# Four PSUM banks for products, two for linear attention's turns, x loaded two blocks ahead, four raw tiles for y

## The chip, the cores and the metric

The kernel runs on one core of a Trainium2 chip. The metric is the device time of one execution in microseconds. Engines: PE is TensorE (matmuls and, with `ident` as one operand, transposes), ACT is ScalarE, DVE is VectorE, POOL is GpSimd, SP is SyncE, whose queue issues nearly all transfers of this kernel. PSUM holds eight banks of 128 x 512 float32; every result of PE lands in one of them and has to be read by another engine before the bank can be written anew.

## The reference

A decoder block with two token mixers side by side, over 2048 tokens of width 1024 and 16 meta tokens set before them:

```python
h = jnp.concatenate([meta, x], axis=1)
u = rms_norm(h, norm_g[l])
proj = u @ w_in[l]
(g_q, g_k, g_v, g_lr, g_z, m_cq, m_ckv, m_kr, m_z,
 gate_gla, gate_mla) = jnp.split(proj, cuts, axis=-1)
gk = jax.nn.log_sigmoid(g_lr @ gla_gate_w[l] + gla_gate_b[l]) / GLA_GATE_NORMALIZER
o_a = gla_chunked(q, k, v, gk)
o_a = rms_norm(o_a, gla_norm_g[l]).reshape(B, L, GLA_VW)
y_a = (o_a * jax.nn.silu(g_z)) @ gla_proj[l]
o_b = mla_attention(m_cq, m_ckv, m_kr, ...)
y_b = (o_b * jax.nn.silu(m_z)) @ mla_proj[l]
merged = jax.nn.sigmoid(gate_gla) * y_a + jax.nn.sigmoid(gate_mla) * y_b
out = rms_norm(h + merged @ w_out[l], final_norm_g)[:, N_META:]
```

`gla_chunked` is linear attention with a decay: a state of 128 x 256 for each of four heads is carried over chunks of tokens. All arithmetic is float32; the kernel splits each operand into a high and a low part (`_hi`, `_lo`) and makes one product of three matmuls (`mm3`, lines 45 to 47).

## The kernel before

Everything is one program for one core. The code is written in an order that follows the data, and a scheduler places the instructions of each engine statically; a tile of a pool can be handed out again when its readers have been placed, so the number of buffers of a pool decides which waits there are.

**Input phase.** `Natural(g)` takes half of the tokens, eight blocks of 128 rows. `norm(b)` loads a block of x and norms it, `turn(b)` transposes it on PE into two banks `pt`, `place(b)` copies these as high and low parts into the operand tiles `y11` to `t4` (ACT and DVE, for some of them POOL). `run()` multiplies the blocks by columns of `w_in` that come in five pieces of about 300 columns: pieces 0 and 1 in a loop over the blocks, beside their loading and placing; pieces 2 to 4 each after the other, over all blocks. `load_w` brings a piece as eight raw tiles, which ACT (`w_hi`, line 171) and DVE (`w_lo`, line 172) convert. A product of a block and a piece is 24 matmuls of 128 x 296 or 304. Here `prep(next)` stands ahead of the two products of a block, so that a block is loaded, normed, turned and placed one turn ahead.

**Pairs.** The other columns of `w_in` go pair by pair: seven products of 12 matmuls of 128 x 512, each in a bank `acc` of the pool `a_ps`. After every product a tick lets the work beside the pairs run a step: first `latents` (MLA's small projections), then `gla`. In the first half (g = 0) latents run beside 8 pairs and `gla` beside 11, in the second beside 5 and 13; one or two pairs remain as a tail.

**Linear attention.** `gla` has 32 units, one for 256 tokens of a head; `FIRST` = 13 of them belong to the first half. A unit is a generator that yields at steps: load q and k; `xp` (the gate, one matmul, in the bank of `b_pm`), then the chain of log-sigmoid, prefix sums and decays up to `kp` on ACT, DVE and POOL; three yields; `kt` (the transposed `kp`, two transposes in the one bank of `b_pt`) with its readers `kt_hi` (ACT) and `kt_lo` (DVE), and `at` (in `b_pm`); then twice `o` and `su` with the state's update; the scale and `on`; two yields; `ot` (four transposes of `on`, again in the bank of `b_pt`). Three to four units are open at a time, so steps of different units stand beside each other.

**GlaProj.** It multiplies y, eight tiles `y` of 128 x 512 for each of four groups of tokens, by `gla_proj`. `load_y` loads a raw tile `y_raw` (two buffers, line 1010) and converts it (`y_hi` on ACT, line 1014; `y_lo` on DVE, line 1015). Three tiles of the next group can be held in advance; the others follow as the last row of products releases their places.

Attention and the output phase come behind and are not touched.

Of the kernel before, what the change touches and what calls it, by code (L numbers as in the profile page):

```python
# [19 lines left out]
P = 128  # L20
# [15 lines left out]
FIRST = 13  # L36
# [115 lines left out]
def phase_ab(tc, ident, x, meta, norm_g, w_in, gate_w, gate_b, gate_b_cols, gnorm_cols, S,  # L152
# [10 lines left out]
    ps = psp("a_ps", 5, space=PSUM)  # L163
# [10 lines left out]
    class Natural:  # L174


        def __init__(self, g):

            self.g, self.right, self.tps = g, Pools(tc, "right"), Pools(tc)
            y12 = self.right("n_y12", 1)  # L180
            self.T = dict(T, y12=[y12.tile([P, KH, 512], F32R, name=f"y12_{e}") for e in ("hi", "lo")])
            self.um = self.right("n_um", 1).tile([P, KC, 3 * M], F32R, name="um") if g == 0 else None
            self.raw = self.right("n_raw", 3)
            self.wa = self.right("n_wa", 1)
            self.xl = Pools(tc, "right")
            self.xin, self.gp = self.xl("n_x", 1), self.xl("n_g", 1)
            self.sm = self.xl("n_sm", 3)
            self.ptr = self.tps("n_pt", 3, space=PSUM)
            self.gb = self.gp.tile([P, D], F32, name="gb")
            self.xt = {}  # L190
            self.order = [8 * g + i + 4 * h for i in range(4) for h in range(2)] + [NB]
            self.norm(8 * g)
            self.w = [self.load_piece(0, self.wa)]
            self.pts = {8 * g: self.turn(8 * g)}

        def norm(self, b):
            rows = P if b < NB else M
            pool = self.xb if self.order.index(b) % 2 else self.xin
            xt = pool.tile([P, D], F32, tag="x", name="xt")
            nc.sync.dma_start(xt[:rows], x[b * P:(b + 1) * P, :] if b < NB else meta)  # L200
            if b == 8 * self.g:
                nc.sync.dma_start(self.gb, norm_g.partition_broadcast(P))
            jk = self.gp.tile([P, D], BF16, tag="jk", name="jk")
# [4 lines left out]
            self.xt[b] = xt  # L208
# [49 lines left out]

        def prep(self, b):
            if b not in self.pts:  # L260
                self.norm(b)
                self.pts[b] = self.turn(b)
            self.place(b)
# [63 lines left out]
        def run(self):  # L327
# [3 lines left out]
            self.xb, self.tmp = tl("n_xb", 1), tl("n_tmp", 1)  # L331
            order = self.order[:8]
            self.place(order[0])
            self.w.append(self.load_piece(1, wb))
            for i, b in enumerate(order):
                if i + 1 < len(order):
                    self.prep(order[i + 1])
                elif g == 0:
                    self.prep(NB)
                for n in range(2):  # L340
                    self.product(b, self.w[n], n)
# [172 lines left out]
    for g in range(2):  # L514
# [6 lines left out]
        n = (8, 5)[g]  # L521
# [20 lines left out]
        active, ticks, total, n = [], 0, 7 * (len(rest) - tail) - 8, len(units)  # L542
# [28 lines left out]
def gla(tc, ident, gate_w, gate_b, gate_b_cols, gnorm_cols, S, group, W=256):  # L571
# [11 lines left out]
    ep = right("b_e", 5)  # L583
# [7 lines left out]
    pt = pps("b_pt", 1, space=PSUM)  # L591
# [92 lines left out]
    def unit(t, h):  # L684
# [9 lines left out]
        xp = pm.tile([P, W], F32, tag="m", name="xp")  # L694
# [30 lines left out]
        for _ in range(3):  # L725
            yield
# [80 lines left out]
def latents(tc, ident, w_uq, w_ukv, gq_cols, gkv, cs, sn, sr, S, group):  # L807
# [6 lines left out]
    pm = pps("l_pm", 1, space=PSUM)  # L814
# [177 lines left out]
class GlaProj:  # L992


    def __init__(self, tc, gla_proj, S):
        self.nc, self.tc, self.S, self.w = tc.nc, tc, S, gla_proj
        self.right, self.psum = Pools(tc, "right"), Pools(tc, "right")
        self.yp = self.right("p_y", 8)
        self.raws = self.right("p_raw", 2)
        self.yr = self.right("p_yr", 2)  # L1000
        self.wa = self.right("p_wa", 1)
        self.ws = {0: self.load_w(0, self.wa)}
        self.pools = [self.yp] * 8
        self.ys = self.load_y(0, range(KC))

    def load_y(self, t, kcs):
        nc, ys = self.nc, []
        for kc in kcs:
            raw = self.yr.tile([P, 512], F32, tag="y", name="y_raw")
# [15 lines left out]
    def steps(self):  # L1025
# [6 lines left out]
        following = self.ys  # L1032
        for t in range(NT):
# [562 lines left out]
```

## Time and profile before

| | us |
|---|---|
| median of three runs | 2673.48 (2671.47 to 2678.76) |
| profiled execution, its own time | 2668.63 |
| its span, first to last instruction | 2666.9 |
| first input loop | 8 to 97 |
| pieces 2 to 4, then pairs with latents | 97 to 365 |
| pairs with linear attention, first part | 365 to 690 |
| second input loop | 690 to 775 |
| pieces 2 to 4, pairs with latents | 775 to 980 |
| pairs with linear attention, second part | 980 to 1310 |
| tail and GlaProj | 1310 to 1560 |
| attention | 1560 to 2300 |
| output | 2300 to 2667 |

A row of the table of stages gives a stretch, its length, and for each engine its busy time with the number of rows in brackets; then the granted clock of PE, where 0.50 is the 1.2 GHz level and 1.00 the 2.4 GHz level, the busy share of the transfer engines and GB/s. In a list of waits each row names the engine with the tile and line that waited, what released it, the total, the number of times and the longest. The idle time of PE counts from the end of a matmul as the profile models it, which lies behind the point where the next could start. In a timeline the columns are the start, the duration, engine, line, operation, output and inputs with their form, and in square brackets the idle time before it with what ended it.

### The profile page before, as it was taken

To read this page: it belongs to the slowest core of one execution; us is meant where nothing else is said; L and a number is where in the kernel's file an instruction comes from. 1 tells how busy PE (TensorE), PEld (TensorE's weight loads), DVE (VectorE), ACT (ScalarE), POOL (GpSimd) and SP (SyncE) were. 2 spreads that over 40 slices of the span, in tenths; PEclk is the share of its full clock that TensorE was granted. 3 is DMA by queue.
4 is the path that set the end of the run, shared out by engine and by line. 5 is a ranking of instruction groups with operands and counts; after the bars stand their busy time and mean duration, and the time that the engine had idled before them with its cause. 6 is when DMAs were issued, how large, how long until landed. Compare 5 with 4: busy or idle time off the path is not lost.

```text
span 2666.9 us, 42612 instructions
## 1 busy us (share of the span) xinstructions
PE 2556.0 (96%) x14873; PEld 2248.9 (84%) x14873; DVE 1597.1 (60%) x3830; ACT 1375.0 (52%) x3242; POOL 441.7 (17%) x413
## 2 busy tenths in 40 slices
PE   7999999889899999999999999999999999999998
PEld 7998777667799777887776888999999999889997
DVE  7434777777652457777533178777776666644333
ACT  5323555665442347567445366665555555544342
POOL 2113543333220221111110010000000000121110
PEclk9999999989999999999999999999999999999999
DMA  5547765656644867777765333111111100454332
GB/s 143 173 148 232 241 217 196 207 190 213 193 126 140 263 212 222 245 225 235 239 210 181 114 121 102 56 60 44 37 44 32 33 29 21 155 162 127 112 122 68
DMA packets 302087, 392.60 MB, mean 147 GB/s; under 512 B 40464, under 2 KB 218944, under 8 KB 301872
## 3 DMA queue, kind: packets, MB, share of 16 engines
q1 hardware_dynamic: 301872, 389.88, 46.1%
q8 instruction: 117, 1.92, 0.3%
q14 instruction: 98, 0.80, 0.1%
HBM read 240.51 MB, written 149.25 MB: 146 GB/s over the span
## 4 chain that ended last, share of the span: by engine, by line
PE 68%; DVE 8%; DMA 8%; ACT 8%; issue 3%; POOL 3%; SPq 1%; DVEq 0%; POOLq 0%; ACTq 0%
PE acc L46 10%; PE acc L47 10%; PE acc L45 10%; PE p_tp L1269 4%; PE o_acc L46 3%; PE o_acc L45 3%; PE o_acc L47 2%; PE s L1217 2%; PE s L1221 2%; PE s L1219 2%; PE s L1220 2%; PE s L1218 2%; PE oacc L47 2%; PE oacc L46 2%; PE oacc L45 2%
## 5 line engine op out<-in xcount | busy, mean ns | idle before, releaser
L45 PE MATMUL acc<-t_hi,xp 128*128 128x512 f32 x640 | 254.9, 398 | 1.0 <-DMA xp<-d_xp 1.0
L47 PE MATMUL acc<-t_hi,xp 128*128 128x512 f32 x640 | 250.9, 392 | 0.4 <-DVE xp L172 0.4
L46 PE MATMUL acc<-t_lo,xp 128*128 128x512 f32 x640 | 250.2, 391 | 0.0
L45 PE MATMUL acc<-w_hi,y_hi 128*128 128x296 f32 (+1 forms) x640 | 196.3, 308 | 2.3 <-ACT w_hi L171 2.3
L46 PE MATMUL acc<-w_lo,y_hi 128*128 128x296 f32 (+1 forms) x640 | 196.5, 307 | 1.7 <-DVE w_lo L172 1.2
L45 PE MATMUL acc<-y_hi,xp 128*128 128x512 f32 x480 | 196.5, 409 | 0.7 <-DMA xp<-d_xp 0.7
L47 PE MATMUL acc<-w_hi,y_lo 128*128 128x296 f32 (+1 forms) x640 | 194.6, 305 | 0.0
L46 PE MATMUL acc<-y_lo,xp 128*128 128x512 f32 x480 | 193.1, 402 | 0.0
L47 PE MATMUL acc<-y_hi,xp 128*128 128x512 f32 x480 | 193.1, 402 | 0.0
L1236 ACT ACTIVATE row<-row,nm,sr 128x144 f32<-128x144 f32 (+15 forms) x128 | 167.3, 1307 | 38.0 <-DVE nm L1235 37.7
L1272 DVE TENSOR_TENSOR p_lo<-p_tp,p_hi 128x512 fp32r<-128x512 f32 x224 | 150.2, 687 | 49.4 <-ACT p_hi L1271 46.8
L1271 ACT ACTIVATE p_hi<-p_tp 128x512 fp32r<-128x512 f32 x224 | 129.3, 594 | 97.8 <-PE p_tp L1269 97.5
L1269 PE MATMUL p_tp<-ident,row 128*128 128x128 f32 x1088 | 168.3, 273 | 0.0
L1223 DVE TENSOR_SCALAR_CACHE_REDUCE row<-s 128x388 f32<-128x388 f32 (+13 forms) x224 | 130.8, 584 | 57.8 <-PE s L1221 55.7
L1322 POOL TENSOR_TENSOR rb<-rb,mz 128x512 f32<-128x512 f32 x32 | 41.3, 1292 | 641.5 <-DMA rb<-d_rl 411.9
L45 PE MATMUL acc<-ob_hi,wp_hi 128*128 128x256 f32 x504 | 142.5, 283 | 3.7 <-ACT wp_hi L987 2.7
L47 PEld LDWEIGHTS acc<-t_hi,xp 128*128 128x128 f32 x640 | 120.2, 188 | 26.4 <-DVE xp L172 0.8
L47 PE MATMUL acc<-ob_hi,wp_lo 128*128 128x256 f32 x504 | 141.9, 282 | 0.1
L46 PE MATMUL acc<-ob_lo,wp_hi 128*128 128x256 f32 x504 | 141.8, 281 | 0.0
L45 PEld LDWEIGHTS acc<-t_hi,xp 128*128 128x128 f32 x640 | 120.6, 188 | 24.4 <-DMA xp<-d_xp 1.0
L1269 PEld LDWEIGHTS p_tp<-ident,row 128*128 128x128 f32 x1088 | 128.8, 140 | 14.3 <-ACT row L1236 4.4
L1217 PE MATMUL s<-kt_hi,q_hi 128*128 128x420 f32 (+16 forms) x352 | 139.3, 396 | 0.5 <-DVE mx L1226 0.5
(339 smaller groups left out, 7527.9 us busy)
## 6 DMA issues: line engine op xcount, KB each, us to landing
d_xp<-xp SPq DMA_DIRECT2D x80, 512.0 KB
xp<-d_xp SPq DMA_DIRECT2D x80, 512.0 KB
w_raw<-in_w_in SPq DMA_DIRECT2D x60, 512.0 KB
xt<-in_x SPq DMA_DIRECT2D x32, 512.0 KB
d_z<-c SPq DMA_DIRECT2D x32, 256.0 KB
v_hi<-d_vh SPq DMA_DIRECT2D x64, 128.0 KB
d_gg<-c SPq DMA_DIRECT2D x32, 256.0 KB
v_lo<-d_vl SPq DMA_DIRECT2D x64, 128.0 KB
```

The lines of the kernel that those rows point to most:

```text
L45: nc.tensor.matmul(out, a_hi, b_hi, start=start, stop=False)
L46: nc.tensor.matmul(out, a_hi, b_lo, start=False, stop=False)
L47: nc.tensor.matmul(out, a_lo, b_hi, start=False, stop=stop)
L1217: nc.tensor.matmul(sv, q_hi[:, js], kt_hi[:, a:b], start=True, stop=False)
L1218: nc.tensor.matmul(sv, q_hi[:, js], kt_lo[:, a:b], start=False, stop=False)
L1219: nc.tensor.matmul(sv, q_lo[:, js], kt_hi[:, a:b], start=False, stop=False)
L1220: nc.tensor.matmul(sv, qa[:, js], kst[:, a:b], start=False, stop=False)
L1223: nc.vector.tensor_scalar(row[:, a:b], sv, 1.0, None, op0=ALU.mult, op1=ALU.max, accum_out=mx[:, i:i + 1])
L1236: nc.scalar.activation(row[:, :w], row[:, :w], AF.Exp, bias=nm, scale=sr[:, 4 * t + j:4 * t + j + 1], accum_out=rl[:, j:j + 1])
L1269: nc.tensor.transpose(tp[:, i, r * P:(r + 1) * P], rws[r][:, M + k * P:M + (k + 1) * P], ident)
L1271: nc.scalar.activation(fl(p_hi), fl(tp), AF.Copy)
L1272: nc.vector.tensor_sub(fl(p_lo), fl(tp), f(fl(p_hi)))
```

## The change

The banks of PSUM are shared out differently. `a_ps` has 4 in place of 5; the pool of `pt` (input phase) 4 in place of 3; `b_pt` 2 in place of 1, and it takes `xp` over from `b_pm`; `l_pm` (latents) 2 in place of 1.

`norm` is divided into `load_x` and `norm`. The first three loads and the second norm stand ahead of the loop, and in each turn of it stand: the norm of the block two ahead, the product with piece 0, turning and placing of the next block, the load of the block three ahead, the product with piece 1.

A unit of linear attention yields four times instead of three between `kp` and `kt`, and the pool of `qe`, `ke`, `kp` has 6 buffers in place of 5. `FIRST` is 12, so that the first half has one unit less and the second one more; the second half's latents stand beside 4 pairs in place of 5, and its linear attention beside 14.

GlaProj gets a second pool of two raw tiles, used in turn with the first once its steps have begun.

```diff
-FIRST = 13
+FIRST = 12
...
-    ps = psp("a_ps", 5, space=PSUM)
+    ps = psp("a_ps", 4, space=PSUM)
...
-            self.ptr = self.tps("n_pt", 3, space=PSUM)
+            self.ptr = self.tps("n_pt", 4, space=PSUM)
...
+            self.load_x(8 * g)
             self.norm(8 * g)
...
-        def norm(self, b):
+        def load_x(self, b):
             rows = P if b < NB else M
             pool = self.xb if self.order.index(b) % 2 else self.xin
-            xt = pool.tile([P, D], F32, tag="x", name="xt")
+            xt = self.xt[b] = pool.tile([P, D], F32, tag="x", name="xt")
             nc.sync.dma_start(xt[:rows], x[b * P:(b + 1) * P, :] if b < NB else meta)
             if b == 8 * self.g:
                 nc.sync.dma_start(self.gb, norm_g.partition_broadcast(P))
+
+        def norm(self, b):
+            rows, xt = P if b < NB else M, self.xt[b]
             jk = self.gp.tile([P, D], BF16, tag="jk", name="jk")
...
+            order = self.order if g == 0 else self.order[:8]
+            self.load_x(order[1])
+            self.place(order[0])
+            self.norm(order[1])
+            self.w.append(self.load_piece(1, wb))
+            self.load_x(order[2])
+            for i, b in enumerate(order):
+                if b == NB:
+                    break
+                nxt = order[i + 1] if i + 1 < len(order) else None
+                if i + 2 < len(order):
+                    self.norm(order[i + 2])
+                self.product(b, self.w[0], 0)
+                if nxt is not None:
+                    self.pts[nxt] = self.turn(nxt)
+                    self.place(nxt)
+                if i + 3 < len(order):
+                    self.load_x(order[i + 3])
+                self.product(b, self.w[1], 1)
             order = self.order[:8]
-            self.place(order[0])
-            self.w.append(self.load_piece(1, wb))
-            for i, b in enumerate(order):
-                if i + 1 < len(order):
-                    self.prep(order[i + 1])
-                elif g == 0:
-                    self.prep(NB)
-                for n in range(2):
-                    self.product(b, self.w[n], n)
...
-        n = (8, 5)[g]
+        n = (8, 4)[g]
...
-        active, ticks, total, n = [], 0, 7 * (len(rest) - tail) - 8, len(units)
+        active, ticks, total, n = [], 0, 7 * (len(rest) - tail) - 11, len(units)
...
-    ep = right("b_e", 5)
+    ep = right("b_e", 6)
...
-    pt = pps("b_pt", 1, space=PSUM)
+    pt = pps("b_pt", 2, space=PSUM)
...
-        xp = pm.tile([P, W], F32, tag="m", name="xp")
+        xp = pt.tile([P, W], F32, tag="t", name="xp")
...
-        for _ in range(3):
+        for _ in range(4):
             yield
...
-    pm = pps("l_pm", 1, space=PSUM)
+    pm = pps("l_pm", 2, space=PSUM)
...
-        self.yr = self.right("p_yr", 2)
+        self.yrs = [self.right("p_yr", 2)]
...
-            raw = self.yr.tile([P, 512], F32, tag="y", name="y_raw")
+            raw = self.yrs[kc // 2 % len(self.yrs)].tile([P, 512], F32, tag="y", name="y_raw")
...
+        self.yrs.append(self.right("p_yr2", 2))
```

The order of instructions on PE in the first linear attention stage, before, around `ot` (the `xp_` with an `acc` is an operand of the pairs; the `xp` of line 695 is the gate's matmul):

```order
L47 MATMUL acc_4887<-y11_hi_330,xp_4768 128x512
L785 MATMUL ot_4907<-ident_315,on_4712 128x128 x4
L45 MATMUL acc_4929<-t1_hi_336,xp_4805 128x512
L46 MATMUL acc_4929<-t1_lo_337,xp_4805 128x512
L47 MATMUL acc_4929<-t1_hi_336,xp_4805 128x512
```

`ot` stands alone between two products. The `xp` of a later unit stands in the second product behind it, behind `o` and `su`:

```order
L47 MATMUL su_4955<-v_hi_4865,kt_lo_4875 128x256
L45 MATMUL acc_4998<-t2_hi_338,xp_4841 128x512
L46 MATMUL acc_4998<-t2_lo_339,xp_4841 128x512
L47 MATMUL acc_4998<-t2_hi_338,xp_4841 128x512
L695 MATMUL xp_4966<-lrT128_4473,gw_4292 128x256
L45 MATMUL acc_4998<-t2_hi_338,xp_4841 128x512
```

The `su` ahead of it is the last use of the one bank of `b_pm` before `xp`. After the change, at the same place of a unit, on PE:

```order
L47 MATMUL acc_4930<-t2_hi_338,xp_4816 128x512
L792 MATMUL ot_4947<-ident_315,on_4793 128x128 x4
L702 MATMUL xp_4964<-lrT128_4498,gw_4292 128x256
L45 MATMUL acc_4996<-t3_hi_340,xp_4851 128x512
L46 MATMUL acc_4996<-t3_lo_341,xp_4851 128x512
L47 MATMUL acc_4996<-t3_hi_340,xp_4851 128x512
```

The gate's `xp` has moved ahead by a product with its `o` and `su`, directly behind `ot`, and takes its bank from the same pool.

On ACT in the same stage, before, from a unit's second `sq` to the next unit's `kt_hi`: `rs_t` and `rs_y` make the scale that `on` needs.

```order
L771 ACTIVATE sq,ssq<-o 128x256
L729 ACTIVATE qs_hi<-qe,dec 128x128
L724 ACTIVATE kp<-ke,dec 128x128 x2
L63 ACTIVATE rs_t<-rs_a 128x2
L729 ACTIVATE qs_hi<-qe,dec 128x128
L64 ACTIVATE rs_y<-rs_t 128x2
L680 ACTIVATE s_hi<-state_4307 128x256
L483 ACTIVATE c_5262<-acc 128x512
L171 ACTIVATE xp<-w_raw 128x512
L775 ACTIVATE on<-o,rs_y 128x256 x2
L171 ACTIVATE xp<-sa 128x512
L741 ACTIVATE kt_hi<-kt 128x256
```

`rs_t` stands behind two copies of `kp` there. On ACT after the change, again to the next `kt_hi`:

```order
L731 ACTIVATE kp<-ke,dec 128x128 x2
L687 ACTIVATE s_hi<-state_4306 128x256
L736 ACTIVATE qs_hi<-qe,dec 128x128 x2
L171 ACTIVATE xp<-sa 128x512
L778 ACTIVATE sq,ssq<-o 128x256
L687 ACTIVATE s_hi<-state_4307 128x256
L63 ACTIVATE rs_t<-rs_a 128x2
L64 ACTIVATE rs_y<-rs_t 128x2
L782 ACTIVATE on<-o,rs_y 128x256 x2
L171 ACTIVATE xp<-w_raw 128x512
L171 ACTIVATE xp<-sa 128x512
L748 ACTIVATE kt_hi<-kt 128x256
```

The copies of `kp` have moved ahead of the second `sq`, and between it and `on` stand only `s_hi`, `rs_t` and `rs_y`; two conversions for the pairs stand between `on` and `kt_hi`, where one stood.

On SP at the start of the second input phase, before: the load of the second block (`xt_8063`) stands among the transfers of piece 1, which are pairs of 168 and 136 columns:

```order
L271 DMA w_raw_8043<-in_w_in 128x168
L271 DMA w_raw_8043<-in_w_in 128x136
L271 DMA w_raw_8048<-in_w_in 128x168
L271 DMA w_raw_8048<-in_w_in 128x136
L200 DMA xt_8063<-in_x 128x1024
L271 DMA w_raw_8053<-in_w_in 128x168
```

Six of piece 1's eight raw tiles are issued ahead of it. On SP after the change, from the first transfer of piece 1 on:

```order
L268 DMA w_raw_7901<-in_w_in 128x168
L201 DMA xt_7875<-in_x 128x1024
L268 DMA w_raw_7901<-in_w_in 128x136
L268 DMA w_raw_7906<-in_w_in 128x168
L411 DMA d_xp19_3_302<-xp_7795 128x1024
L268 DMA w_raw_7906<-in_w_in 128x136
L475 DMA d_gm7_113<-c22_7812 128x512
L268 DMA w_raw_7911<-in_w_in 128x168
L268 DMA w_raw_7911<-in_w_in 128x136
L201 DMA xt_7941<-in_x 128x1024
```

The second block's load (`xt_7875`) has moved behind the first transfer of piece 1, and the third's (`xt_7941`) stands eight places behind it, ahead of most of the piece.

## Rows read from the trace of the kernel before

**Rows 1.** Table of stages: stretch, length, busy PE, PEld, DVE, ACT, POOL, clock, transfers.

```profile
0.00:97.00 97.00, 80.40 (x551) 76.94 (x552) 65.13 (x135) 53.16 (x128) 24.99 (x22) 0.98 0.48 133
97.00:172.00 75.00, 75.00 (x553) 74.56 (x552) 23.21 (x49) 20.10 (x49) 5.17 (x4) 1.00 0.56 172
...
365.00:690.00 325.00, 290.99 (x1367) 232.52 (x1366) 236.54 (x498) 182.04 (x474) 106.69 (x96) 0.95 0.63 208
```

**Rows 2.** What PE waited for, 0 to 100 us: total, times, longest.

```profile
PE pt L217 <- DVE xt L207: 15.2, 4, 8.4
```

**Rows 3.** What PE waited for, 365 to 690 us.

```profile
PE ot L785 <- DVE kt_lo L742: 11.3, 5, 3.8
PE xp L695 <- DVE state L767: 6.5, 6, 3.7
PE kt L739 <- ACT kp L724: 6.1, 4, 2.5
...
PE ot L785 <- ACT on L775: 2.2, 1, 2.2
...
PE pt L217 <- DVE xt L207: 1.6, 1, 1.6
```

**Rows 4.** What PE waited for, 690 to 790 us.

```profile
PE pt L217 <- DVE xt L207: 6.9, 3, 3.6
PE acc L45 <- ACT w_hi L171: 2.1, 3, 1.2
```

**Rows 5.** What PE waited for, 975 to 1310 us.

```profile
PE kt L739 <- ACT kp L724: 2.3, 1, 2.3
PE xp L695 <- DVE state L767: 1.6, 2, 1.0
```

**Rows 6.** What PE waited for, 1395 to 1510 us.

```profile
PE acc L45 <- ACT y_hi L1014: 6.1, 6, 1.5
PE acc L46 <- DVE y_lo L1015: 1.1, 5, 0.2
```

**Rows 7.** Half-clock stretches, sums: four behind `ot`; two behind `xp`, `kt`; input loop; GlaProj.

```profile
441.40:448.20 6.80, 6.09 (x17) 4.93 (x18) 3.46 (x8) 0.94 (x2) 1.28 (x1) 0.50 0.84 272
...
sum 20.40, PE 17.85 PEld 14.55 DVE 12.37 ACT 9.76 POOL 3.84; mean PE 4.46 PEld 3.64 DVE 3.09 ACT 2.44 POOL 0.96
...
sum 10.20, PE 8.49 PEld 6.96 DVE 7.03 ACT 7.25 POOL 0.12; mean PE 4.24 PEld 3.48 DVE 3.52 ACT 3.62 POOL 0.06
...
707.60:717.80 10.20, 8.64 (x28) 6.22 (x27) 5.75 (x15) 5.80 (x17) 0.00 (x0) 0.50 0.73 216
...
sum 10.20, PE 9.13 PEld 6.91 DVE 3.64 ACT 5.40 POOL 0.00; mean PE 4.57 PEld 3.45 DVE 1.82 ACT 2.70 POOL 0.00
```

**Rows 8.** Timeline, 436 to 443 us, of PE, DVE, POOL and ACT.

```profile
436.09 0.48 PE L45 MATMUL acc<-t_hi,xp 128*128 128x512 f32 x1
...
438.69 0.39 PE L47 MATMUL acc<-t_hi,xp 128*128 128x512 f32 x1
442.11 1.12 PE L785 MATMUL ot<-ident,on 128*128 128x128 f32 x4 [3.04 <-DVE kt_lo L742]
...
437.01 1.24 DVE L66 TENSOR_TENSOR rs_t<-rs_t,rs_a 128x2 f32<-128x2 f32 x1
...
441.64 0.42 DVE L742 TENSOR_TENSOR kt_lo<-kt,kt_hi 128x256 fp32r<-128x256 f32 x1
...
436.49 1.74 POOL L491 TENSOR_TENSOR c<-c,c 128x512 f32<-128x512 f32 x1 [1.57 <-DVE rs_t L65]
...
439.64 0.84 ACT L775 ACTIVATE on<-o,rs_y 128x256 f32<-128x256 f32 x2 [3.69 <-DVE rs_y L68]
```

**Rows 9.** Timeline, end of the second input loop, PE and POOL.

```profile
763.23 1.03 PE L217 MATMUL pt<-ident,xt 128*128 128x128 f32 x8
...
770.39 2.54 POOL L172 TENSOR_TENSOR t_lo<-f,t_hi 128x512 fp32r<-128x512 f32 x2
```

**Rows 10.** Timeline, ACT in GlaProj.

```profile
1404.53 0.63 ACT L1014 ACTIVATE y_hi<-y_raw 128x512 fp32r<-128x512 f32 x1 [1.88 <-DMA y_raw<-d_y]
```

More of the change, by code (lines that the diff above doesn't have):

```diff
@@ L207, in norm @@
             nc.vector.scalar_tensor_tensor(xt[:rows], xt[:rows], rstd, self.gb[:rows], op0=ALU.mult, op1=ALU.mult)
-            self.xt[b] = xt
         def turn(self, b):
@@ L257, in place @@
             split(part("t4"), t4, nc.gpsimd)
[L259 to L263, printed above, removed]
         def load_w(self, pool, pieces, width):
```

## The prediction

> **What bounds the kernel now.** I read the table of stages first, then what TensorE (PE) waited for in each stage, then the stretches with a low granted clock, then the timeline at single stalls. The reader should see that PE is the bound almost everywhere: in the stretch 97 to 172 us it is busy all the time, 75.00 us with 553 rows of matmuls, 0.136 us for each [rows 1]. Stages that the change touches are those where it is not: the first input loop (80.40 of 97 us) and linear attention beside the pairs (290.99 of 325 us in the first of its two stages) [rows 1]. Attention and output, behind 1560 us, have the same order of instructions after the change as before; I put nothing there.
>
> The waits name the culprits. In the first input loop PE waits for normed blocks: 15.2 us in 4 waits, of which 8.4 is the start of the kernel, where nothing has been loaded; 6.8 are left [rows 2]. In the second it is 6.9 us for blocks and 2.1 for weights [rows 4]. In the first linear attention stage `ot` waits 11.3 us for `kt_lo`, which must be read before the one bank can be written again, and 2.2 for `on`; `xp` waits 6.5 for a reader of the one bank of `b_pm`, and `kt` waits 6.1 for `kp` [rows 3]. In the second, `kt` and `xp` wait 3.9 together [rows 5]. GlaProj waits 6.1 for `y_hi` and 1.1 for `y_lo` [rows 6].
>
> A second loss hangs on the first. After several of the longer waits the granted clock stands at 0.50, the 1.2 GHz level, for some 3.4 or 6.8 us [rows 7]. Work in such a stretch takes twice its time, so half of the stretch's busy part is lost: a wait of 3 us costs some 5.
>
> **The change part by part.** All sums are against the profiled execution, 2668.6 us; the median of the three runs lies 4.9 above it, and I add that at the end.
>
> *First input loop.* Every block is loaded and normed one turn earlier than before. Nothing is added on PE. I expect the 6.8 us [rows 2] to go. On the other side the last turn now stands 24 matmuls closer to the first product that needs piece 2: 24 x 0.136 = 3.3 us less cover for `w_hi` and `w_lo` of piece 2, whose conversion stands behind the placing of the last block on ACT (ScalarE) and DVE (VectorE). In this loop the trace has no wait for piece 2, so part of the 3.3 is covered. I take -5, bounds -6.8 and 0.
>
> *Second input loop.* SyncE (SP) issues block 2 ahead of the weights of piece 1 and block 3 among the first of them, so the 6.9 us of [rows 4] go, and so does a wait of the same kind that the first block of this loop has (1.6 us [rows 3]). The clock is at 0.50 from 707.6 to 717.8 us with 8.64 us of matmuls [rows 7]: 4.3 us are lost. It follows waits for the weights of piece 1, and these the change loads no sooner; I give half of it, 2. At the end of the loop stands the opposite: the last turn at 763.23 [rows 9] is followed by two GpSimd (POOL) operations `t_lo`, 2.54 us together from 770.39 [rows 9], and only then ACT comes to `w_hi` of piece 2, for which PE already waits. The 3.3 us of lost cover show here, I take 2 of them. Sum -6.9 - 1.6 - 2 + 2 = -8.5; bounds -15 (all waits and all of the clock) and -3 (the clock stays, 3.3 and one block's wait come back).
>
> *First linear attention.* Three things happen to a unit. The distance from `xp` to its own `kt` grows from 32 to 48 matmuls of products; 11 steps from 436.09 to 438.69 us take 2.60, 0.236 each [rows 8], so 3.8 us more, and the longest wait of `kt` for `kp` was 2.5 us; the 6.1 us go. `xp` leaves `b_pm`, so its wait for the state update, 6.5, loses its reason. And with two banks `ot` no longer waits for `kt_lo`, but `xp`, which now stands directly behind `ot`, takes the bank of the `kt` issued one product earlier, and so waits for the same `kt_lo`, later only by the four transposes of `ot`. The price of that new wait is not in the trace. Its lower bound is nought; its upper one is the wait of `ot` itself. What was late in the stall at 442 us: `on` began at 439.64 and took 0.84, `kt_lo` began at 441.64, and PE stood still for 3.04 us [rows 8]. `ot` needs `on` in any case. On ACT, though, the scale of `on` (`rs_t`, `rs_y`) stands behind the two copies of `kp` before, and directly behind the second `sq` after, so `on` and with it `kt_hi` should come sooner. So: 6.1 + 6.5 of waits go; of the clock the stretch at 530.1 followed the longest `xp` wait, and one of 3.4 us at 567.6 the longest `kt` wait; the two hold 8.49 us of matmuls [rows 7], half is 4.2. That makes 16.8. The `ot` part is 11.3 + 2.2 and, for the clock in the four stretches behind its longer waits, half of 17.85 [rows 7], which is 8.9: 22.4 in all. I take a seventh of it, 3, since the same tile is still waited for in the same place. Sum -20; bounds -8 (`kt` and its clock alone) and -39 (all).
>
> What can hold `on` and `kt_lo` back: DVE needed 1.24 us at 437.01 for an operation on 2 columns, while POOL's addition of 1.74 us ran from 436.49 [rows 8]; the `kt_lo` of 256 columns took 0.42. The Trainium skill, "SBUF — State Buffer", section "SBUF: two separate sides", says that DVE and GpSimd share one pair of ports under an exclusive lock held for a whole instruction, and that the loser blocks. This trace agrees (1.24 against 0.42). By that rule the lateness belongs to POOL's additions of the pairs, which the change leaves in place, so that `kt_lo` stays late and only the waiting instruction changes its name; the sum would then be that of rival (a).
>
> *Second linear attention.* The same move, -2.3 - 1.6 [rows 5]; one unit more runs here and one less in the first stage, over one pair more, and the latents before it get four pairs in place of five. No row shows that denser mix. The nearest is the longest single stall of this stage, 2.3 [rows 5]; I bound it by nought and three of these, 7, and take 1, since PE has the same products to lay between. Sum -3, bounds -4 and +3.
>
> *GlaProj.* Before, two raw tiles: a load starts when its tile has been converted, and ACT waits 1.88 us for one [rows 10]. With four, two to three loads are under way while the last one is converted. The load itself is no longer than before; 7.2 us of PE waits [rows 6] go and, of the clock in the two stretches behind them, half of 9.13 [rows 7]: 7.2 + 4.6 = 11.8. I take -11, bounds -7 and -13.
>
> *One acc bank less.* Four products in flight instead of five. No wait of PE in the pairs' stages is for the reader of an `acc` bank [rows 3, 5]; three products of 12 matmuls, 8.5 us at 0.236 each, still lie between a bank's last matmul and its next first. I take nothing, bounds 0 and +3, one stall such as the longest here. `l_pm` with two banks: nothing, since the latents show no wait for it.
>
> Sum: -5 - 8.5 - 20 - 3 - 11 = -47.5. 2668.6 - 47.5 = 2621, and with 4.9 a median of **2626**.
>
> **The rivals.**
> (a) *The wait is renamed.* `xp` behind `kt_lo` takes over what `xp` and `ot` waited for; only `kt` gains. For it: POOL's additions beside the pairs stay where they are, and the 1.24 us on DVE with them [rows 8]. (The rule of the Trainium skill on the shared ports, in "SBUF — State Buffer", speaks for this rival.) Against it: `on` moved forward on ACT. First linear attention -8 in place of -20: **2638**.
> (b) *All stalls of the touched stages go*, clock included: -6.8 - 15 - 39 - 4 - 13 = -78, **2596**. For it: short waits leave the clock high, so that gains multiply. Against: the wait for `kt_lo` stays in the code.
> (c) *Slower.* The new wait of `xp` decides: it is hit in every one of 12 units, at the mean of the five waits before (11.3/5 = 2.3 [rows 3]), with a clock loss of 1.7, half a stretch of 3.4 us, behind each: 12 x 4.0 = 48, while the other terms and `kt` bring 28 + 8 = 36. That is +12, **2685**. It decides from 3.0 us per unit. Against it: before, only 5 of 13 units waited here.
> (d) *The loops do not gain.* The blocks come earlier, but the loads compete with the piece's weights and both loops pay 3.3 for lost cover: +6.6 in place of -13.5, **2646**. For it: weights are already late in the second loop, 2.1 us. Against it: they are little beside the 6.9 for blocks [rows 4].
>
> **How the numbers follow.** The forecast has 0.48, (a) 0.20, (b) 0.14, (d) 0.10, (c) 0.08. With all terms at one end the sum is -78, at the other -12 (0, -3, -8, +3, -7, +3), and since they are not likely to fall to one side together, the forecast's own range is half the way to each: 2611 to 2643. The whole range has to reach over (a) and (d) and to the edge of (b): 2598 to 2654. Faster by over 0.3%, 8 us, about what a measurement of this kernel can tell from no change: 0.88. Within it: 0.06, parts of (c) and (d). Slower: 0.06.
>
> **What would show it.** In the new profile the table of stages should end the first linear attention some 20 us sooner and GlaProj 11 sooner. In the waits of PE, those for `xt` should be at most 3 us besides the start, `kt` for `kp` near nought, `ot` for `on` and `xp` for `kt_lo` at most 10 together. `acc` waiting for an eviction would make the bank term wrong; `xp` for `kt_lo` over 12 us means (a); over 36 with its clock, (c); `acc` for `w_hi` above 5 us at the end of the loops, (d). No stretch at 0.50 near 1410 is wanted; if one stays, the GlaProj term is too large.

## The result

The changed kernel takes 2645.65 us (median of four runs, 2642.73 to 2647.87), the one before 2676.12 in the same comparison: a ratio of 0.9897, 95% interval 0.988 to 0.9914. That is some 27.5 us by the ratio and 30.5 by these medians. The forecast was 2626, with a range of 2598 to 2654: the direction and the range held, and the gain is a little over half of the 47.5 us in the forecast's sum.

Where the time went, by the places of the products (a stage ends where PE starts the first product of the next; the first one begins with PE's first instruction), in us of the profiled executions. The middle column is the kernel with four raw tiles for y alone, whose instructions stand in the same order as before up to the y products; what differs there, up to 7 us in a stage, is what two executions differ by.

| stage | before | y tiles alone | after |
|---|---|---|---|
| first loop | 79.8 | 82.5 | 78.3 |
| its pieces 2 to 4 | 87.8 | 87.5 | 88.9 |
| 8 pairs with latents | 186.7 | 193.6 | 185.2 |
| first linear attention | 337.6 | 335.2 | 320.1 |
| second loop | 77.0 | 77.5 | 68.3 |
| its pieces 2 to 4 | 79.7 | 79.2 | 83.9 |
| second latents and linear attention | 493.9 | 496.2 | 498.6 |
| y products | 192.7 | 185.1 | 185.5 |
| attention and output | 1115.3 | 1115.8 | 1115.5 |

The first linear attention after the change, as a row of the table of stages (stretch, length, busy PE, PEld, DVE, ACT, POOL, clock, transfers), and what PE waited for there (total, times, longest):

```profile
365.00:662.00 297.00, 268.57 (x1294) 217.18 (x1295) 221.93 (x465) 170.86 (x442) 103.16 (x90) 0.97 0.66 215
```

```profile
PE o L45 <- ACT sq L778: 13.3, 7, 3.0
PE su L45 <- DVE state L774: 6.2, 3, 2.8
...
PE ot L792 <- DVE kt_lo L749: 1.0, 1, 1.0
...
PE xp L702 <- DVE kt_lo L749: 0.5, 1, 0.5
```

Against [rows 3] the wait of `kt` is gone, that of `xp` has gone from 6.5 to 0.5 and that of `ot` from 11.3 to 1.0. In their place stand `o` for `sq`, 13.3 us, and `su` for the state, 6.2. All idle time of PE in the stage together fell only from 33.9 to 29.6 us (37.0 in the trace with y tiles alone).

The granted clock is 0.97, where it was 0.95 [rows 1]. That the change raised it is not shown: the trace with y tiles alone has the same order on PE and ACT in this stage as the one before, and it stands at 0.97 too. The stage there, as a row of the table of stages:

```profile
372.20:707.50 335.30, 298.18 (x1423) 238.23 (x1423) 246.45 (x513) 186.86 (x483) 109.55 (x99) 0.97 0.64 209
```

One such wait of `o`, in the timeline (start, duration, engine, line, operation; in brackets the idle time before and what ended it):

```profile
531.01 0.45 ACT L120 ACTIVATE ab<-xp,gcols 128x256 f32<-128x256 f32 x1
...
536.55 0.21 ACT L712 ACTIVATE dec<-b 128x4 f32<-128x4 f32 x1 [1.28 <-DVE b L706]
537.45 0.42 ACT L725 ACTIVATE eq<-bc 128x256 f32<-128x256 f32 x1 [0.68 <-POOL bc L723]
537.77 0.40 ACT L726 ACTIVATE ek<-bc 128x256 f32<-128x256 f32 x1
538.08 0.40 ACT L687 ACTIVATE s_hi<-state 128x256 fp32r<-128x256 f32 x1
538.38 0.36 ACT L778 ACTIVATE sq<-o 128x256 f32<-128x256 f32 x1
...
536.80 0.61 POOL L723 TENSOR_TENSOR bc<-b,mid 128x256 f32<-128x256 f32 x1 [1.44 <-DVE mid L710]
...
538.89 0.39 PE L45 MATMUL o<-v_hi,a_hi 128*128 128x256 f32 x1 [3.00 <-ACT sq L778]
...
534.30 1.62 DVE L465 TENSOR_TENSOR c<-c,e_st 128x512 f32<-128x512 f32 x1
...
536.63 0.47 DVE L774 SCALAR_TENSOR_TENSOR state<-state,dd,su 128x256 f32<-128x256 f32 x1
...
533.87 1.50 POOL L409 TENSOR_TENSOR sa<-w_raw,sb 128x512 f32<-128x512 f32 x1 [5.97 <-ACT ab L122]
```

On ACT `sq`, whose input was there at about 533, ran behind the gate chain of a younger unit: `ab` from the new place of `xp`, then `dec`, `eq` and `ek`, of which `eq` waits for POOL's `bc`. `o` started at 538.89, when `sq` was done.

The order on ACT is not all of it. This `o` also needs `s_hi`, which ACT makes from the state, and DVE had the state ready only at 537.10. On DVE it ran behind the prefix sum and behind an operation of line 465 that took 1.62 us beside a sum of weights (`sa`) on POOL; the same line took 0.69 at 530.31. So some 1.2 of the 3.0 us, from 535.89 to 537.10, would have stood with any order on ACT.

In the second loop after the change no wait for `xt` is left; PE waits for these:

```profile
PE acc L45 <- ACT w_hi L171: 2.5, 3, 1.2
PE acc L47 <- DVE y_lo L172: 2.3, 2, 1.4
PE acc L45 <- DMA w_raw<-in_w_in: 2.3, 1, 2.3
```

The last turn and the first products with piece 2, PE, same loop:

```profile
738.53 1.04 PE L220 MATMUL pt<-ident,xt 128*128 128x128 f32 x8
...
751.91 0.41 PE L45 MATMUL acc<-w_hi,y_hi 128*128 128x296 f32 x1 [1.16 <-ACT w_hi L171]
...
755.07 0.41 PE L45 MATMUL acc<-w_hi,y_hi 128*128 128x296 f32 x1 [0.66 <-ACT w_hi L171]
```

Against [rows 9] the turn stands closer to piece 2, and two waits for `w_hi` of piece 2 follow, 1.8 us together. Before there was none: the three waits for `w_hi` in [rows 4] stand at 705 to 712 us and are for piece 1. The products of y wait less than in [rows 6], but one long wait is left. First PE's waits, then PE and ACT in the timeline:

```profile
PE acc L45 <- ACT y_hi L1021: 4.2, 3, 3.1
...
1430.30 0.50 PE L45 MATMUL acc<-y_hi,p_hi 128*128 128x512 f32 x1 [3.05 <-ACT y_hi L1021]
...
1427.24 0.42 ACT L1152 ACTIVATE wv_hi<-ldv 128x256 fp32r<-128x256 f32 x1 [1.69 <-DMA ldv<-in_w_ukv]
...
1429.10 0.63 ACT L132 ACTIVATE gg<-gg 128x512 f32<-128x512 f32 x1 [0.58 <-DMA gg<-d_gg]
1429.63 0.61 ACT L1021 ACTIVATE y_hi<-y_raw 128x512 fp32r<-128x512 f32 x1
```

`y_hi` was late at 1429.63 not for a load but behind work of attention's start on ACT, whose `wv_hi` waited for its own transfers until 1427.24, and `gg` until 1429.10; no load of `y_raw` was issued between 1395 and 1431 us.

### The profile page after: what moved, and what is told of

It reads as the page before. It is cut to its first block, busy times and chain, and to the rows that moved or that the text cites. A ratio compares the mean times of both kernels' runs of the same rounds, so it can differ in the third digit from the quotient of the medians.

```text
span 2641.0 us, 42616 instructions
## 1 busy us (share of the span) xinstructions
PE 2546.1 (96%) x14871; PEld 2243.7 (85%) x14871; DVE 1589.6 (60%) x3829; ACT 1372.6 (52%) x3241; POOL 441.1 (17%) x409
## 4 chain that ended last, share of the span: by engine, by line
PE 49%; DMA 5%; ACT 4%; DVE 3%; issue 1%; POOL 1%; SPq 0%; DVEq 0%; POOLq 0%; ACTq 0%
PE acc L45 5%; PE acc L47 5%; PE acc L46 5%; PE p_tp L1277 4%; PE o_acc L46 3%; PE o_acc L45 3%; PE o_acc L47 3%; PE s L1225 2%; PE s L1229 2%; PE s L1227 2%; PE s L1228 2%; PE s L1226 2%; PE oacc L47 2%; PE oacc L46 2%; PE oacc L45 2%
## 5 line engine op out<-in xcount | busy, mean ns | idle before, releaser
L45 PE MATMUL acc<-y_hi,xp 128*128 128x512 f32 x480 | 193.6, 403 | 0.2 <-DMA xp<-d_xp 0.2
L47 PE MATMUL acc<-y_hi,xp 128*128 128x512 f32 x480 | 190.4, 397 | 0.0
```

The lines of the kernel that those rows point to most:

```text
L45: nc.tensor.matmul(out, a_hi, b_hi, start=start, stop=False)
L47: nc.tensor.matmul(out, a_lo, b_hi, start=False, stop=stop)
```

## The experiments

My theory after the result: the change removed the waits that it aimed at, and what ACT, DVE and POOL deliver late came back under other names, since their order and speed stayed. The rival: the new order on ACT alone makes the new waits. For the loops: lost cover against late weights. Ratios are to the kernel before in the same comparison, with the 95% interval. There were three such comparisons behind the result, in which the kernel before took 2674.78, 2674.32 and, for `e11_adds_before` and the last three runs of this section, 2678.97 us; differences of medians across them are uncertain by some 4 us, and the ratio is then the better guide.

**Input phase alone**, `e1_input`. The kernel before with these parts of the diff:

```diff
-    ps = psp("a_ps", 5, space=PSUM)
+    ps = psp("a_ps", 4, space=PSUM)
-            self.ptr = self.tps("n_pt", 3, space=PSUM)
+            self.ptr = self.tps("n_pt", 4, space=PSUM)
...
+                self.product(b, self.w[0], 0)
+                if nxt is not None:
+                    self.pts[nxt] = self.turn(nxt)
+                    self.place(nxt)
```

> The kernel before with the input phase of the change alone (loads and norms two blocks ahead, four banks for pt, four for products). Theory from the two traces: in the new loop the next block is turned between a block's two products, so its placing has 24 matmuls (3.3 us) of cover in place of 48, and the products wait for y_hi and y_lo instead of for xt; the two loops then bring 0 and -4.5 us, so some -4 to -6 in all against before, with waits for y_lo of piece 0 of 1 us and more late in each loop. Rival, the forecast: the waits for xt go and nothing comes back, -13 us. Fewer product banks cost nothing by both; if they cost, the pairs' stages grow by 3 us or more.

0.9981 (0.9967 to 0.9995), 4 us by the medians and 5 by the ratio. The second loop is 4.9 us shorter than before and its pieces 3.9 longer; the first loop 0.5 shorter, its pieces 1.6 longer. What PE waited for in the second loop:

```profile
PE acc L47 <- DVE y_lo L172: 1.6, 2, 1.4
PE acc L45 <- ACT y_hi L171: 1.1, 1, 1.1
PE pt L220 <- DVE xt L211: 0.7, 1, 0.7
```

The waits for `xt` fall from 6.9 to 0.7, those for `y_lo` and `y_hi` come, and with 2.3 for `w_lo` and 2.1 for `w_hi` the weights stay as late as before: the theory on the loops, not the forecast. The stages of the pairs with linear attention did not grow (334.0 and 493.8 us); the 8 pairs with latents took 188.9 in place of 186.7, within what two executions differ by. No `acc` waited for its bank's reader: one bank less costs nothing.

**Four raw tiles alone**, `e2_yraw`.

```diff
-        self.yr = self.right("p_yr", 2)
+        self.yrs = [self.right("p_yr", 2)]
...
+        self.yrs.append(self.right("p_yr2", 2))
```

> The kernel before with four raw tiles for y alone. By the two traces the stretch of the y products is 7 us shorter after the change, so -7; by the forecast -11, waits of PE for y_hi below 1 us in all and no stretch at half clock there. If the gain needs the other parts (other transfers at that time), it is under 3 us.

0.9972 (0.996 to 0.9983), 7.5 us (6.7 by the medians); the stage is 7.6 shorter, as in the changed kernel (7.2). So the gain does not need the other parts. The forecast of -11 fails here too: `y_hi` is still waited for 3.2 us, not under 1, and one stretch of 3.4 us at half clock is left.

**One step less**, `e3_step3`. The changed kernel with this, and with the buffers and the count of ticks that belonged to three steps:

```diff
-        for _ in range(4):
+        for _ in range(3):
             yield
```

> The changed kernel with three yields again between kp and kt (and five buffers for qe, ke, kp), the two banks of b_pt kept. The gate's xp then stands behind o and su of an older unit again. Theory: what the second o waits for (13.3 us for sq in the first stage after the change) is the gate chain of a younger unit, which stands ahead of sq on ACT since xp moved ahead; here that wait falls below 4 us, kt waits for kp again for about 6 us, and the time is within 5 us of the changed kernel. Rival: the wait for sq comes from DVE and POOL holding each other up, wherever xp stands; then it stays above 9 us, the kt wait comes on top, and the kernel is 8 us or more slower than the changed one.

0.9913 (0.9894 to 0.9932) against 0.9897 of the changed kernel: about the same. In the first linear attention, 324.7 us:

```profile
PE ot L792 <- ACT on L782: 6.7, 2, 4.9
PE pt L220 <- DVE xt L211: 5.5, 1, 5.5
...
PE o L45 <- ACT sq L778: 2.9, 2, 1.6
```

The wait for `sq` falls from 13.3 to 2.9, as the theory of the order on ACT wanted. But `kt` hardly waited again (0.6 in all); `ot` waits for `on` instead, 6.7. The name moves with the order, the time hardly: 5.5 of the 324.7 us are one wait of the second loop's first turn for its block, which the changed kernel has not, and without it the stage takes 319.2, against 320.1.

**The step inside the chain**, `e5_split`. The changed kernel with

```diff
+        yield
         b = wt("b")
         nc.vector.tensor_tensor_scan(b, keep, g, 0.0, op0=ALU.mult, op1=ALU.add)
...
-        for _ in range(4):
+        for _ in range(3):
             yield
```

> The changed kernel with one of the four yields moved to between log-sigmoid and the prefix sum, so that xp stays directly behind ot, while the prefix sum, the decays and kp are written a step later, behind o and sq of the older unit. Theory: the wait of the second o for sq falls from 13.3 us in the first stage to below 5, that of su for the state from 6.2 to below 3, and the kernel is 8 to 15 us faster than the changed one. Rival, late DVE and POOL in themselves: both waits stay within a quarter of what they were, and the time is within 4 us.

0.9884 (0.9858 to 0.991): not to be told from the changed kernel's 0.9897. First linear attention 316.3 us:

```profile
PE o L45 <- ACT s_hi L687: 5.0, 3, 3.2
PE o L45 <- ACT sq L779: 3.4, 2, 2.6
```

`sq` falls to 3.4 and `su` for the state is no longer on the list, both as expected; `s_hi` takes 5.0. The stage gains 3.8 of the 8 to 15, and that is no more than executions differ by: in `e6_turn`, whose order on PE here is that of the changed kernel, it takes 323.0 in place of 320.1. So the order on ACT names the wait and sets little of the time.

**Turning ahead of both products**, `e6_turn`. The changed kernel with

```diff
-                self.product(b, self.w[0], 0)
                 if nxt is not None:
                     self.pts[nxt] = self.turn(nxt)
                     self.place(nxt)
+                self.product(b, self.w[0], 0)
```

> The changed kernel with the turning and placing of the next block written ahead of both products of a block, as in the kernel before; loads and norms stay two blocks ahead. Theory: the loops gave back what they won because placing had only 24 matmuls of cover; here the waits for y_hi and y_lo in the loops (4.6 us together after the change) go, those for w_hi of piece 2 fall by 2 us or more, no wait for xt comes back, and the two loops with their pieces are 5 to 9 us shorter than after the change. Rival: what is lost at the end of the loops comes from the weights' transfers and not from the cover; then the pieces behind the loops stay as long as after the change and the gain is under 3 us.

0.9884 (0.9864 to 0.9905), again not to be told from the changed kernel. Second loop, PE's waits:

```profile
PE acc L45 <- ACT w_hi L171: 3.1, 3, 2.1
PE acc L46 <- DVE w_lo L172: 1.6, 2, 0.8
PE pt L220 <- issue: 1.5, 1, 1.5
```

`y_lo` and `y_hi` are gone, and the pieces behind the loop fall from 83.9 to 80.8 us: cover was the cause there. But waits for `xt` came back, 1.3 us, and `w_hi` of piece 2 still waits 0.9 of 1.8. The loop itself grew from 68.3 to 70.8, since the second block's turn now stands ahead of its first product. Both loops with their pieces are 2.1 us shorter (317.3 against 319.4), not 5 to 9.

**13 units in the first half**, `e4_first13`. The changed kernel with

```diff
-FIRST = 12
+FIRST = 13
-        n = (8, 4)[g]
+        n = (8, 5)[g]
```

> The changed kernel with 13 units of linear attention in the first half and five pairs beside the second latents, as before. Both theories: the unit's own 20 small matmuls (3 to 4 us) move back to the first half. If the redistribution is neutral, the sum of both linear attention stages with the second latents stays within 3 us of the changed kernel; if the denser second latents cost what they seemed to (8 us over five pairs, of which a unit's steps are a part), this one is 4 us or more faster; if the first half is the crowded one, 3 us or more slower.

0.9867 (0.9852 to 0.9883), 2638.92 us: 7 us under the changed kernel, with intervals that just overlap. The second latents with linear attention take 490.4 us in place of 498.6, the first 321.7 in place of 320.1. All four runs lie under all four of the changed kernel. So this part of the change cost some 6 us, the moved unit's own matmuls in the second half included. Whether the moved unit or the latents beside four pairs cost it stays open, since this run undoes both.

**A pair's additions on DVE**, `e7_adds`. The changed kernel with

```diff
-            nc.gpsimd.tensor_add(c22, c12, c21)
-            nc.gpsimd.tensor_add(c12, c12, u2)
+            nc.vector.tensor_add(c22, c12, c21)
+            nc.vector.tensor_add(c12, c12, u2)
```

> The changed kernel with the two additions of a pair that POOL makes (c22 and c12) put on DVE. The rule of the Trainium skill, SBUF - State Buffer, section SBUF: two separate sides, makes these additions the cause of late DVE work. By it, DVE operations of 2 columns no longer take over 1 us beside them, the waits of PE for sq, state and s_hi in the first linear attention stage (21 us after the change) fall by a third or more, and the kernel is 5 to 10 us faster. By the other theory, order on ACT, the waits stay and DVE, with 1.2 us more work for each pair of additions, makes it 0 to 8 us slower.

0.9798 (0.9783 to 0.9814), 2621.01 us: 24 us under the changed kernel, over twice the upper end of what the rule on the ports was expected to give. First linear attention 308.5 us in place of 320.1, second with latents 486.0 in place of 498.6. `su` for the state falls from 6.2 to 0.5 us; `o` for `sq` stays at 11.6. The third that was expected of these waits is there, but the stage gained more than the waits fell. DVE's operations in the stage, 365 to 660 us (line, engine, operation, count, then busy and mean ns, idle before):

```profile
L498 DVE TENSOR_TENSOR c<-c,c 128x512 f32<-128x512 f32 x11 | 11.4, 1033 | 0.0
...
L706 DVE TENSOR_TENSOR_SCAN b<-keep,g 128x256 f32<-128x256 f32 x12 | 11.2, 932 | 0.3
L499 DVE TENSOR_TENSOR c<-c,u 128x512 f32<-128x512 f32 x11 | 10.8, 986 | 0.1
```

The sign that the rule was to give did not come in this stage. The prefix sum still takes 932 ns (953 after the change). Four operations of 2 columns still take over 1 us, as after the change, and in both traces each of the four lies beside a sum of weights on POOL, none beside an addition. Counted against the fastest operation of the same form, DVE's operations in the stage are longer by 34.6 us in all, and after the change by 39.7. The 5 us between are under half of the 11.6 that the stage gained; where the rest comes from stays open. In the second half, where POOL makes no sums, the same count falls from 25.3 to 9.8 us, and the stage gains 12.6.

**The same on the kernel before**, `e11_adds_before`, the same edit.

> The kernel before with a pair's two additions (c22, c12) on DVE in place of POOL, nothing else. If POOL's additions are what made DVE and with it kt_lo, on and state late, this edit works without the change too: 20 us or more faster than before, with the waits of ot for kt_lo and of xp for the state (17.8 us in the first linear attention stage) more than halved. If the gain of 24 us on the changed kernel needs the change's free banks and steps, it is under 12 us here and ot goes on waiting for kt_lo.

0.9843 (0.9828 to 0.9857): two lines that the change left alone bring 42 us, more than the change. By the traces 22.3 of it are in the first linear attention and 11.3 in the second with its latents. PE's waits in the first linear attention, 315.3 us in place of 337.6:

```profile
PE xp L695 <- DVE state L767: 6.8, 7, 1.9
PE ot L785 <- ACT on L775: 4.4, 2, 3.4
PE ot L785 <- DVE kt_lo L742: 4.3, 4, 1.8
...
PE kt L739 <- ACT kp L724: 2.9, 2, 1.7
```

Beside [rows 3], `ot` for `kt_lo` falls from 11.3 to 4.3 and `kt` for `kp` from 6.1 to 2.9, with one bank still; `xp` for the state stays (6.8), so that the two expected to be halved go from 17.8 to 11.1. `ot` for `on` has 4.4 in place of 2.2. Of nine operations of 2 columns on DVE that took over 1 us in this stage before, four lay beside an addition on POOL, two of them in the stall of [rows 8]; those four are gone, and four are left, each beside a sum of weights. Much of the lateness was upstream of the banks.

**Split step and early turn**, `e9_both`, the two edits of `e5_split` and `e6_turn` together.

> The changed kernel with the yield moved to between log-sigmoid and the prefix sum, and the turning of the next block ahead of both products. If both theories hold, some 4 us in linear attention and 5 to 9 us in the input loops add up: 9 to 13 us faster than the changed kernel, a ratio to the kernel before of 0.985 to 0.9865. If the order of the waits is all that changes, within 4 us of the changed kernel.

0.986 (0.9839 to 0.9882), 2637.98 us: 8 under the changed kernel by the medians, short of the 9 to 13; the ratio lies within the expected 0.985 to 0.9865. Both are beyond the 4.

**Additions on DVE and 13 units**, `e13_adds13`.

> The changed kernel with the additions of a pair on DVE, and with 13 units in the first half and five pairs beside the second latents. The two edits alone gave 24 and 7 us against the changed kernel; if they are independent, 2612 to 2617 us. If the 13 units gained because they moved work away from POOL's additions, the sum is smaller: 2618 to 2622.

0.9775 (0.9757 to 0.9792), 2619.58 us. Against `e7_adds` that is 1.4 us by the medians, which come from two comparisons, and 6 by the ratios (0.9798 and 0.9775), whose intervals overlap. Whether the 7 us of the 13 units are still there on top of the additions stays open.

**All of these**, `e10_all`.

> The same as the run with additions on DVE and 13 units, and besides the yield ahead of the prefix sum and the turning ahead of both products, which together gave 8 us on the changed kernel. If what they take away is not the lateness that the additions caused, 2605 to 2612 us, and the waits of o for sq in the first linear attention stage (11.6 us with the additions on DVE) fall below 5. If it is the same lateness, within 4 us of the run without them.

0.9763 (0.9747 to 0.9779), 2614.4 us, 5 under the run before it: between the two expectations. The wait for `sq` is 6.0, not under 5; the run before it had 7.5.

**The weights' sums on DVE too**, `e12_sums`. The last one with

```diff
-            add, sub = nc.gpsimd.tensor_add, nc.gpsimd.tensor_sub
+            add, sub = nc.vector.tensor_add, nc.vector.tensor_sub
```

> The last one with the sums of weights of the pairs (sa, sb; 100 operations of 1.3 to 1.5 us on POOL) on DVE as well. If any POOL operation beside DVE costs as the additions did, another 5 to 15 us faster. If DVE, busy for some 70 per cent of the linear attention stages, is then the one that is waited for, slower by up to 10 us.

0.9655 (0.9638 to 0.9672), 2585.76 us, the fastest of all: 28.6 us under the run before it, about twice the upper end of what was expected, and 60 under the changed kernel. What is left of the wait for `sq`, and the first linear attention's stretch:

```profile
PE o L45 <- ACT sq L779: 2.0, 2, 1.7
PE o L46 <- DVE s_lo L688: 1.7, 3, 0.6
...
365.00:660.00 295.00, 285.39 (x1433) 235.54 (x1433) 244.46 (x586) 182.91 (x485) 14.32 (x28) 0.99 0.73 236
```

PE is busy for 285.39 of 295 us, DVE for 244.46: more work on DVE, and little waiting for it. The stage takes 294.3 us, and none of its operations of 2 columns on DVE takes over 1 us.

How long an operation took, 365 to 660 us, in the changed kernel (line, engine, operation, count, then busy and mean ns, idle before), the last row POOL's addition of the pairs:

```profile
L706 DVE TENSOR_TENSOR_SCAN b<-keep,g 128x256 f32<-128x256 f32 x12 | 11.4, 953 | 0.3
...
L127 DVE TENSOR_TENSOR g<-g,ab 128x256 f32<-128x256 f32 x12 | 6.9, 572 | 3.8 <-ACT ab L122 3.4
...
L749 DVE TENSOR_TENSOR kt_lo<-kt,kt_hi 128x256 fp32r<-128x256 f32 x12 | 5.0, 418 | 1.3 <-ACT kt_hi L748 1.2
...
L499 POOL TENSOR_TENSOR c<-c,u 128x512 f32<-128x512 f32 x11 | 15.7, 1427 | 0.6
```

and in the last kernel, the last row that addition on DVE, over the whole run:

```profile
L707 DVE TENSOR_TENSOR_SCAN b<-keep,g 128x256 f32<-128x256 f32 x13 | 8.9, 685 | 0.1
...
L750 DVE TENSOR_TENSOR kt_lo<-kt,kt_hi 128x256 fp32r<-128x256 f32 x13 | 5.5, 420 | 1.4 <-ACT kt_hi L749 1.4
L127 DVE TENSOR_TENSOR g<-g,ab 128x256 f32<-128x256 f32 x13 | 5.4, 419 | 0.3
...
L499 DVE TENSOR_TENSOR c<-c,u 128x512 f32<-128x512 f32 x40 | 27.4, 686 | 0.3
```

The prefix sum falls from 953 to 685 ns and `g` from 572 to 419, while `kt_lo`, which reads `kt` in PSUM, stays at 418 and 420. The addition takes 686 ns on DVE and 1427 on POOL. The Trainium skill, "SBUF — State Buffer", section "Who interferes with whom", says that a DVE instruction with two SBUF inputs contends with a POOL instruction that reads SBUF; the rows agree, for of the operations shown those that lengthen read both inputs from SBUF and `kt_lo` doesn't. That sentence does not cover `rs_a`, which reads one input from SBUF, `ssq`, and took 1.09 to 1.22 us three times in the changed kernel's stage. By the count used for `e7_adds`, DVE's operations in this stage are longer than their fastest by 6.3 us here, against 34.6 there: most of that hung on the sums, not on the additions. How much of the 60 us is that, and how much is that the same addition takes half the time on DVE or that `bc` no longer stands behind POOL's other work, these runs don't tell apart.

## Why the prediction was right or wrong

**First loop, forecast -5.** Wrong in size: -0.5 with its pieces, and `e1_input` gives +1. The waits for `xt` went, but the step "nothing is added on PE" left out that the new order halves the cover of every placing, not only that at the end: `y_lo` and `rs_a` came in their place.

**Second loop, -8.5.** The loop gave 8.7; its pieces gave 4.2 back, where I had put 2. In sum -4.5. The 8.7 come near the 8.9 that the sum had for the loop (6.9 of waits, 2 of clock) by luck. PE's idle time in it fell by 3.3 us, from 9.0 to 5.7, since a wait of 2.3 for a load of weights and 2.7 for `y_lo` and `y_hi` came in; the clock gave more than the 2, with 0.91 before and 0.98 after. And that PE already waited for `w_hi` of piece 2 before was misread: those waits are for piece 1.

**First linear attention, -20.** -17.5 by the two traces, -15 against the second trace of the same order (335.2), and one unit less is in it. So near to -20 it came partly by luck: the sum does not have the unit's own matmuls (3 to 4 us by the estimate of `e4_first13`), and of the clock's part nothing is shown, since 17.1 us of the stage stood at half clock after the change and as many in the second trace of the same order, against 34.1 in the first. The waits of `kt`, `xp` and `ot` fell from 26.1 to 1.5, so rival (a) is wrong by its letter: `xp` waits 0.5 for `kt_lo`. It is right in its core: the late work behind them stayed and was renamed, to `o` for `sq` and `su` for the state, 19.5 together. I had followed `on` forward on ACT and not what the moved gate chain now stood ahead of, the `sq` of the older unit, nor what DVE gave late.

**Second linear attention, -3.** Wrong: +4.7 together with its latents (+2.4 against the second trace). One part that was to go stayed, the wait of `kt`, 2.3 us in [rows 5]:

```profile
PE kt L746 <- ACT kp L731: 2.0, 1, 2.0
```

And `e4_first13` shows that the moved unit and the denser latents cost some 6 us, where I had put +1: that step failed. The unit's own matmuls are in it, and 10.2 us at half clock stand in the stage, where the trace before has none.

**GlaProj, -11.** -7.2, and -7.5 alone. The step that failed is that all 7.2 us of waits were the load's: 4.9 are left, 4.2 for `y_hi` and 0.7 for `y_lo`, and 3 of them are one wait behind attention's first work on ACT. The clock's part held: 13.7 us of the stage stood at half clock before, 3.4 after.

**One bank less, 0.** Right, by `e1_input`.

**Rival (a) and the rule behind it.** It named POOL's additions as what holds the stage, and moving them helps: `e11_adds_before` takes 22 us from the first linear attention by them alone. That they do it by lengthening DVE's operations, as the rule has it, is shown in part: four long operations beside additions went in `e11_adds_before`, but most of the lengthening in this stage lies beside POOL's sums of weights, which the prediction did not name, and went only in `e12_sums`. Its consequence was wrong: not `xp` was held, but the whole chain on ACT and DVE, under whatever name.

**The number.** 2645.65 lies just outside the forecast's own range, 2611 to 2643, and on rival (d)'s 2646. This does not bear (d) out: it had the loops at +6.6, and they brought -5.0; linear attention and GlaProj, which it took over from the forecast, fell short.

In sum -0.5 - 1.5 (latents) - 17.5 - 4.5 + 4.7 - 7.2 + 0.2 = -26, as the two profiled executions differ. The errors nearly all lie on one side, since each term took the removal of a wait for the removal of its cause.

## What to carry to other kernels

A wait that a bank or a buffer ends has two sides: who holds it and why the holder is late. Before giving it more banks, look along the late engine's queue for what runs long or stands in front; here POOL's additions of 1.4 us were worth moving, which brought more than the whole change (0.9843 against 0.9897); both, with the sums moved too and smaller edits, gave 0.9655. When a generator's step is moved, list what its operations now stand ahead of on every engine, and check the cover of each thing that moved, not only of the one meant.

## What was not expected of the hardware

Putting 80 additions and 80 sums on an engine that was busy for 75% of a stage (221.93 of 297 us) made that stage faster (320.1 to 294.3 us, with smaller edits among it and one unit more in the stage) and raised that share only to 83% (244.46 of 295). Two executions of the same instructions differ by up to 7 us in one stage (186.7 and 193.6), so that a term of 3 us can't be read from one pair of traces.
